# Linear attention on one core: longer load runs, one pool for PSUM tiles, a block-diagonal second matmul, and another order and another issuer at the end

The kernel runs on one core of a Trainium2 chip. The metric is the device time of one execution in microseconds (us), smaller being better.

## The reference

For each of 8 x 12 heads, with 512 rows of 64 numbers:

```python
Q_feat = np.maximum(0, Q) + 1
K_feat = np.maximum(0, K) + 1
KV = np.einsum('bhkd,bhkv->bhdv', K_feat, V)
K_sum = np.sum(K_feat, axis=2)
numerator = np.einsum('bhqd,bhdv->bhqv', Q_feat, KV)
denominator = np.einsum('bhqd,bhd->bhq', Q_feat, K_sum)
return (numerator / (denominator[:, :, :, None] + 1e-10)).astype(np.float32)
```

Q, K, V and the result are fp32 of 12.58 MB each, so 37.75 MB must be read and 12.58 MB written.

## The kernel before

It works in 12 groups of 4096 rows. Each group has three loads of 1.05 MB of fp32 that are cast to bf16 on the way (all but the first K), and one fp32 store of 1.05 MB. A *run* is the piece that is contiguous in memory: with `c` rows of 64 fp32 values per partition, 2 KB for `C = 8` and 4 KB for `C2 = 16`.

```python
C = 8; C2 = 2 * C; NP = 4; NG = 12; D1 = D + 1; W = 2 * D + 1
def view(t, c):
    return t.flatten_outer_dims().rearrange("(n p c) d -> p n c d", p=P, c=c)
q_dram = view(Q, C2); k_dram = view(K, C); v_dram = view(V, C); o_dram = view(out, C)
# ... pools; PSUM: qt 2 x 1 bank, kva 1 x 2 banks, out 2 x 2 banks

def load(g):       # K, V, Q of one group; k_raw of group 0 on nc.sync, all else on nc.gpsimd
    nc.gpsimd.dma_start(out=k_raw, in_=k_dram[:, g * NP : g * NP + NP])
    nc.gpsimd.dma_start(out=v_raw, in_=v_dram[:, g * NP : g * NP + NP])
    nc.gpsimd.dma_start(out=q_raw, in_=q_dram[:, g * 2 : g * 2 + 2])
def store(g):
    nc.gpsimd.dma_start(out=o_dram[:, g * NP : g * NP + NP], in_=outs.pop(g))

def features(g):          # VectorE: max(x + 1, 1) of K and Q; ScalarE: V into v_aug
    ...                   # beside columns of ones
def kv_and_transpose(g):  # 32 matmuls 64x128x129 into kva_ps, copied to kva (ScalarE);
    ...                   # 16 transposes of qf, copied to qt (ScalarE)
def output(g):            # h of 2: 32 matmuls of 64x64x65 into two PSUM tiles, then
    ...                   # for each tile reciprocal and multiply on VectorE into o_sb

for it in range(NG + 2):
    if it < NG: features(it)
    if 1 <= it < NG + 1: kv_and_transpose(it - 1)
    if it >= 2: output(it - 2)
    if it + IN_BUFS < NG: load(it + IN_BUFS)      # IN_BUFS = 4
    if it - LAG >= 0: store(it - LAG)             # LAG = 3
# ... the last store
```

`features`, `kv_and_transpose` and `output` each hand work to several engines. In the traces each engine's instructions stand in the order in which they are emitted: VectorE's part of output(9), for example, comes right behind the last Q feature, at 108.08 us. PSUM is the memory that holds the results of matmuls until they are copied out.

## Time and profile before

| | before |
|---|---|
| time, median of the first 3 runs | 131.68 us (130.78 to 132.09) |
| span of the profiled execution | 129.8 us |
| read + written | 37.75 + 12.58 MB, 388 GB/s over the span |
| busiest engine | ScalarE, 48% |
| DMA engines | 9 tenths or more from slice 2 to 37 of 40 |

In lines of the profile PE is TensorE (PEld its weight loads), DVE is VectorE, ACT is ScalarE, POOL is GpSimd and SP is SyncE; L93 is line 93 of that kernel, and `a<-b` says that a is written and b read. The prediction shows the busy shares, the slices and the end. Two more lines are of use. They are from the view of waits (engine and line, what was waited for: us in total, times, longest):

```profile
DVE qf L93 <- DMA q_raw<-in_Q_dram: 42.2, 12, 5.4
...
POOL out_dram L90 <- DVE o_sb L165: 19.6, 3, 10.2
```

The first is VectorE waiting for Q in each of the 12 groups: a fast engine behind a slow supply, which costs nothing as such. The second is the opposite: GpSimd could not issue three stores because the results were not there. It happens only at the end, and there the supply of work to the DMA engines is what is late.

These lines are the DMA view (packets in total; then by queue and kind, with packets, MB, and share of the 16 engines' span):

```profile
DMA packets 19213, 32.17 MB, mean 248 GB/s; under 512 B 768, under 2 KB 12544, under 8 KB 19200
...
q8 instruction: 10, 0.16, 0.5%
```

The 12,544 packets under 2 KB are mostly those of the K and V loads: 1 KB written for a run of 2 KB read. The line of queue 8 is for later: ten transfers of 16 KB that bring instructions.

### The profile page before, as it was taken

The page shows a single profiled execution, that of the slowest core. Times are in us where ns is not written, and L with a number is a line of the kernel's source. Part 1 is how long each engine was busy: PE and PEld are TensorE (multiplying, and loading weights), DVE is VectorE, ACT ScalarE, POOL GpSimd, SP SyncE. Part 2 cuts the span into 40 slices and gives each one's busy share as a digit, 9 for nine tenths or more (in the row PEclk, how much of TensorE's full clock was granted, in tenths as well). Part 3 has the DMA queues.
Part 4 walks back from the last instruction along what each step waited for, and adds up shares of the span by engine and source line. Part 5 has one row for each costly group of instructions (what it writes and reads, how often), then busy time and mean ns, then how long its engine had stood idle before and what let it go on. Part 6 is the DMA issues. An engine that isn't in the chain of part 4 may idle for free.

```text
span 129.8 us, 3048 instructions
## 1 busy us (share of the span) xinstructions
PE 59.0 (46%) x1344; PEld 50.5 (39%) x1344; DVE 57.7 (44%) x132; ACT 62.6 (48%) x73; POOL 36.1 (28%) x55
## 2 busy tenths in 40 slices
PE   0008309208758292864939119409606802933200
PEld 0007209107647191753828009308505701922100
DVE  0222212057374775727577077066227407567700
ACT  3023086590966939296690590391095096270000
POOL 6972224222332242224224222422231200202020
PEclk9999965555686959555595865875785685595555
DMA  2999999999999999999999999999999999999853
GB/s 93 321 204 195 210 194 204 210 206 211 205 209 208 209 207 206 210 207 207 277 302 207 253 331 205 231 350 191 218 347 223 212 357 418 420 417 360 341 218 121
DMA packets 19213, 32.17 MB, mean 248 GB/s; under 512 B 768, under 2 KB 12544, under 8 KB 19200
## 3 DMA queue, kind: packets, MB, share of 16 engines
q0 software_dynamic: 18672, 30.94, 106.3%
q1 hardware_dynamic: 528, 1.05, 2.1%
q8 instruction: 10, 0.16, 0.5%
q14 instruction: 3, 0.02, 0.0%
HBM read 37.75 MB, written 12.58 MB: 388 GB/s over the span
## 4 chain that ended last, share of the span: by engine, by line
DMA 72%; issue 19%; POOL 4%; POOLq 1%
DMA out_dram<-o_sb 31%; DMA k_raw<-in_K_dram 16%; DMA q_raw<-in_Q_dram 15%; DMA v_raw<-in_V_dram 9%; POOL out_dram L90 2%; POOLq L219 1%; POOL q_raw L86 1%; POOL k_raw L82 0%; POOL v_raw L85 0%; POOL identity masks.py:199 0%; POOL identity masks.py:197 0%; POOL v_aug L179 0%; POOLq L90 0%; POOLq L86 0%; POOLq L208 0%
## 5 line engine op out<-in xcount | busy, mean ns | idle before, releaser
L104 ACT COPY v_aug<-v_raw 128x1024 bf16<-128x1024 bf16 x24 | 24.1, 1056 | 48.6 <-DMA v_raw<-in_V_dram 48.6
L152 PE MATMUL o_ps<-kva,qt 64*64 64x65 bf16 x768 | 17.3, 229 | 46.9 <-DVE o_sb L165 45.8
L165 DVE TENSOR_TENSOR o_sb<-o_ps,recip 128x512 f32<-128x512 f32 x48 | 33.2, 691 | 1.6
L152 PEld LDWEIGHTS <-qt 64*64 64x64 bf16 x768 | 12.7, 137 | 52.0 <-DVE o_sb L165 48.9
L139 ACT COPY qt<-qt_ps 128x1024 bf16<-128x1024 bf16 x24 | 29.5, 1298 | 0.4
L118 PE MATMUL kva_ps<-v_aug,kf 64*128 64x129 bf16 x384 | 22.3, 302 | 15.4 <-ACT v_aug L104 10.1
L93 DVE TENSOR_SCALAR qf<-q_raw 128x2048 bf16<-128x2048 bf16 x12 | 8.3, 694 | 42.2 <-DMA q_raw<-in_Q_dram 42.2
L118 PEld LDWEIGHTS <-kf 64*128 64x128 bf16 x384 | 19.1, 137 | 16.2 <-issue 15.6
L138 PE MATMUL qt_ps<-identity,qf 128*128 128x128 bf16 x192 | 21.7, 303 | 0.1
L90 POOL DMA_DIRECT2D out_dram<-o_sb x12 | 9.3, 774 | 38.2 <-DVE o_sb L165 19.6
L138 PEld LDWEIGHTS <-qf 128*128 128x128 bf16 x192 | 18.8, 142 | 2.6 <-issue 2.2
L93 DVE TENSOR_SCALAR kf<-k_raw 128x1024 bf16<-128x1024 bf16 (+1 forms) x24 | 9.8, 450 | 11.2 <-DMA k_raw<-in_K_dram 11.1
L164 DVE RECIPROCAL recip<-o_ps 128x8 f32<-128x8 f32 x48 | 9.6, 201 | 10.5 <-PE o_ps L152 10.5
L85 POOL DMA_DIRECT2D v_raw<-in_V_dram x12 | 9.1, 759 | 17.0 <-ACT kva L127 5.4
L82 POOL DMA_DIRECT2D k_raw<-in_K_dram x11 | 8.6, 786 | 16.7 <-DVE kf L93 6.6
L86 POOL DMA_DIRECT2D q_raw<-in_Q_dram x12 | 8.4, 702 | 15.9 <-DMA k_raw<-in_K_dram 9.0
L127 ACT CAST kva<-kva_ps 64x260 bf16<-64x260 f32 x24 | 8.8, 367 | 3.5 <-PE kva_ps L118 3.4
L104 ACT ACT_TABLE_LOAD x1 | 1.3, 1283 | 0.7 <-PEq L208 0.7
masks.py:199 POOL TENSOR_SCALAR_AFFINE_SELECT identity<-identity 128x128 bf16<-128x128 bf16 x1 | 0.3, 287 | 0.1
masks.py:197 POOL MEMSET identity<- 128x128 bf16 x1 | 0.2, 244 | 0.0
L179 POOL MEMSET v_aug<- 128x16 bf16 x2 | 0.2, 175 | 0.0
L208 POOL MEMSET const-float32-0.0<- 128x1 f32 x1 | 0.1, 99 | 0.2 <-issue 0.2
(3 smaller groups left out, 0.3 us busy)
## 6 DMA issues: line engine op xcount, KB each, us to landing
out_dram<-o_sb POOLq DMA_DIRECT2D x12, 1024.0 KB, 20.0
v_raw<-in_V_dram POOLq DMA_DIRECT2D x12, 512.0 KB, 19.7
q_raw<-in_Q_dram POOLq DMA_DIRECT2D x12, 512.0 KB, 19.8
k_raw<-in_K_dram POOLq DMA_DIRECT2D x11, 512.0 KB, 19.7
k_raw<-in_K_dram SPq DMA_DIRECT2D x1, 1024.0 KB, 5.0
```

What stands on the lines that cost most here:

```text
L85: nc.gpsimd.dma_start(out=v_raw, in_=v_dram[:, g * NP : g * NP + NP])
L86: nc.gpsimd.dma_start(out=q_raw, in_=q_dram[:, g * 2 : g * 2 + 2])
L90: nc.gpsimd.dma_start(out=o_dram[:, g * NP : g * NP + NP], in_=outs.pop(g))
L93: nc.vector.tensor_scalar(out=dst, in0=src, scalar1=1.0, scalar2=1.0, op0=ALU.add, op1=ALU.max)
L104: nc.scalar.copy(out=va[:, h].rearrange("p c (n x) -> p n c x", n=2)[:, :, :, 0:D], in_=v_raw[:, h:NP:2],)
L118: nc.tensor.matmul(kva_ps[:, j, h * W : h * W + W], lhsT=kf[64 * j : 64 * j + 64, h, c, :, :], rhs=va[64 * j : 64 * j + 64, h, c, 0:W], st ...
L127: nc.scalar.copy(out=kva[64 * n : 64 * n + 64, :, :, 0:D1], in_=kva_ps[64 * n : 64 * n + 64, :, 0 : 2 * W].rearrange("p j (h x) -> p j h x ...
L138: nc.tensor.transpose(qt_ps[:, c, :], qf[:, half * C + c, :, :], identity)
L139: nc.scalar.copy(out=qt[:, :, :, half], in_=qt_ps)
L152: nc.tensor.matmul(ops[n][64 * j : 64 * j + 64, c // 4, off : off + D1], lhsT=qt[64 * n : 64 * n + 64, c, 32 * b : 32 * b + 32, :], rhs=kv ...
L164: nc.vector.reciprocal(out=recip, in_=den)
L165: nc.vector.tensor_tensor(out=o_sb[:, 2 * n + h].rearrange("p (b r) d -> p b r d", b=2), in0=num, in1=recip.to_broadcast([P, 2, 4, D]), op ...
```

## The change

Its intent: K and V in runs of 4 KB as Q has them; one block-diagonal matmul of 128 rows in place of two of 64 for each pair of heads; PSUM tiles from one pool of three; and an order of their own for the last two groups, so that VectorE's work on the third last outputs does not stand behind the last loads. The last store goes in two halves on SyncE. With these come seven output buffers for six, the features of Q in two halves, and four copies of the first matmuls' result for two. The diff is shortened (`...`).

```diff
-OUT_BUFS = 6
+OUT_BUFS = 7
-    k_dram = view(K, C)
-    v_dram = view(V, C)
+    k_dram = view(K, C2)
+    v_dram = view(V, C2)
+    psum = ... tile_pool(name="psum", bufs=3, PSUM)      # for kva_ps and o_ps; psum_kva, psum_out go
+    kva_diag = [const.tile([P, 4, 2, D1], BF16, ...) for i in range(NV)]   # zeroed once
     def store(g):
+        if g < NG - 1:
+            nc.gpsimd.dma_start(out=o_to, in_=o_sb)
+            return
+        for h in range(2):
+            nc.sync.dma_start(out=o_to[:, h:NP:2], in_=o_sb[:, h:NP:2])
     def kv_and_transpose(g):
-        # h, c of 8, j of 2: 64-row matmuls
+        # c of 16, b of 4: 32-row matmuls, one head each
+                ps = slice(32 * b, 32 * b + 32)
+                nc.tensor.matmul(kva_ps[b // 2][:, b % 2, 0:W], lhsT=kf[ps, c, :, :], rhs=va[ps, c, :], ...)
     def output(g):
-        lhsT=qt[64 * n : 64 * n + 64, c, 32 * b : 32 * b + 32, :], rhs=kva[64 * n : 64 * n + 64, j, h, 0:D1]
+        lhsT=qt[:, c, 32 * b : 32 * b + 32, :], rhs=kva[:, b]
# ...
-        for it in range(NG + 2): ...
+        for g in range(NG - 1):
+            # features(g), kv_and_transpose(g - 1), output(g - 2), load, store as before
+        kv_and_transpose(NG - 2)
+        output(NG - 3)
+        features(NG - 1)
+        output(NG - 2)
+        kv_and_transpose(NG - 1)
+        output(NG - 1)
+        for g in range(NG - 1 - LAG, NG):
+            store(g)
```

More of the change, by code (lines that the diff above doesn't have):

```diff
@@ L13 @@
 BANK = 512
-VP = 130
 IN_BUFS = 4
-OUT_BUFS = 6
+OUT_BUFS = 7
 LAG = 3
@@ L44 @@
     D1 = D + 1
-    W = 2 * D + 1
+    W = 2 * D1
     def view(t, c):
@@ L61 @@
     recip_pool = ctx.enter_context(tc.tile_pool(name="recip", bufs=4))
+    psum = ctx.enter_context(tc.tile_pool(name="psum", bufs=3, space=bass.MemoryType.PSUM))
     psum_qt = ctx.enter_context(tc.tile_pool(name="psum_qt", bufs=2, space=bass.MemoryType.PSUM))
-    psum_kva = ctx.enter_context(tc.tile_pool(name="psum_kva", bufs=1, space=bass.MemoryType.PSUM))
-    psum_out = ctx.enter_context(tc.tile_pool(name="psum_out", bufs=2, space=bass.MemoryType.PSUM))
     identity = const.tile([P, P], BF16, name="identity")
     NV = 2
-    v_aug = [const.tile([P, 2, C, VP], BF16, name=f"v_aug{i}") for i in range(NV)]
+    v_aug = [const.tile([P, C2, W], BF16, name=f"v_aug{i}") for i in range(NV)]
+    kva_diag = [const.tile([P, 4, 2, D1], BF16, name=f"kva_diag{i}") for i in range(NV)]
     raw = {}
     feat = {}
-    mid = {}
+    qts = {}
     outs = {}
@@ L77, in load @@
         k_raw = (head_pool if first else in_pool).tile(
-            [P, NP, C, D], FP32 if first else BF16, name="k_raw"
+            [P, 2, C2, D], FP32 if first else BF16, name="k_raw"
         )
-        v_raw = in_pool.tile([P, NP, C, D], BF16, name="v_raw")
+        v_raw = in_pool.tile([P, 2, C2, D], BF16, name="v_raw")
         q_raw = in_pool.tile([P, 2, C2, D], BF16, name="q_raw")
         (nc.sync if first else nc.gpsimd).dma_start(
-            out=k_raw, in_=k_dram[:, g * NP : g * NP + NP]
+            out=k_raw, in_=k_dram[:, g * 2 : g * 2 + 2]
         )
-        nc.gpsimd.dma_start(out=v_raw, in_=v_dram[:, g * NP : g * NP + NP])
+        nc.gpsimd.dma_start(out=v_raw, in_=v_dram[:, g * 2 : g * 2 + 2])
         nc.gpsimd.dma_start(out=q_raw, in_=q_dram[:, g * 2 : g * 2 + 2])
@@ L89, in store @@
     def store(g):
-        nc.gpsimd.dma_start(out=o_dram[:, g * NP : g * NP + NP], in_=outs.pop(g))
+        o_sb = outs.pop(g)
+        o_to = o_dram[:, g * NP : g * NP + NP]
+        if g < NG - 1:
[3 more added lines that the diff above has]
+            nc.sync.dma_start(out=o_to[:, h:NP:2], in_=o_sb[:, h:NP:2])
     def feature(dst, src):
@@ L98, in features @@
         k_raw, v_raw, q_raw = raw.pop(g)
-        kf = feat_pool.tile([P, 2, C, 2, D], BF16, name="kf")
+        kf = feat_pool.tile([P, C2, 2, D], BF16, name="kf")
         qf = feat_pool.tile([P, C2, 2, D], BF16, name="qf")
         va = v_aug[g % NV]
-        for h in range(2):
-            feature(kf[:, h].rearrange("p c n d -> p n c d"), k_raw[:, h:NP:2])
+        for half in range(2):
+            cs = slice(half * C, half * C + C)
+            feature(kf[:, cs].rearrange("p c n d -> p n c d"), k_raw[:, :, cs])
             nc.scalar.copy(
-                out=va[:, h].rearrange("p c (n x) -> p n c x", n=2)[:, :, :, 0:D],
-                in_=v_raw[:, h:NP:2],
-            )
-        feature(qf.rearrange("p c n d -> p n c d"), q_raw)
+                out=va[:, cs].rearrange("p c (n x) -> p n c x", n=2)[:, :, :, 0:D],
+                in_=v_raw[:, :, cs],
+            )
+        for half in range(2):
+            cs = slice(half * C, half * C + C)
+            feature(qf[:, cs].rearrange("p c n d -> p n c d"), q_raw[:, :, cs])
         feat[g] = (kf, qf)
@@ L113, in kv_and_transpose @@
         va = v_aug[g % NV]
-        kva_ps = psum_kva.tile([P, 2, BANK], FP32, name="kva_ps")
-        for h in range(2):
-            for c in range(C):
-                for j in range(2):
-                    nc.tensor.matmul(
-                        kva_ps[:, j, h * W : h * W + W],
-                        lhsT=kf[64 * j : 64 * j + 64, h, c, :, :],
-                        rhs=va[64 * j : 64 * j + 64, h, c, 0:W],
-                        start=(c == 0),
-                        stop=(c == C - 1),
-                    )
-        kva = mid_pool.tile([P, 2, 2, D1 + 1], BF16, name="kva")
-        for n in range(2):
-            nc.scalar.copy(
-                out=kva[64 * n : 64 * n + 64, :, :, 0:D1],
-                in_=kva_ps[64 * n : 64 * n + 64, :, 0 : 2 * W].rearrange(
-                    "p j (h x) -> p j h x", h=2
-                )[:, :, :, D * n : D * n + D1],
-            )
+        kva_ps = [psum.tile([P, 2, BANK], FP32, tag="ps", name="kva_ps") for _ in range(2)]
+        for c in range(C2):
+            for b in range(4):
+                ps = slice(32 * b, 32 * b + 32)
+                nc.tensor.matmul(
+                    kva_ps[b // 2][:, b % 2, 0:W],
+                    lhsT=kf[ps, c, :, :],
+                    rhs=va[ps, c, :],
+                    start=(c == 0),
+                    stop=(c == C2 - 1),
+                )
+        kva = kva_diag[g % NV]
+        for n in range(2):
+            ps = slice(64 * n, 64 * n + 64)
+            for h in range(2):
+                nc.scalar.copy(
+                    out=kva[ps, 2 * h : 2 * h + 2, n, :],
+                    in_=kva_ps[h][ps, :, D1 * n : D1 * n + D1],
+                )
         qt = mid_pool.tile([P, C, P, 2], BF16, name="qt")
@@ L139, in kv_and_transpose @@
             nc.scalar.copy(out=qt[:, :, :, half], in_=qt_ps)
-        mid[g] = (kva, qt)
+        qts[g] = qt
     def output(g):
-        kva, qt = mid.pop(g)
+        kva = kva_diag[g % NV]
+        qt = qts.pop(g)
         o_sb = out_pool.tile([P, NP, C, D], FP32, name="o_sb")
         for h in range(2):
-            ops = [psum_out.tile([P, 2, BANK], FP32, tag="o_ps", name="o_ps") for _ in range(2)]
+            ops = [psum.tile([P, 2, BANK], FP32, tag="ps", name="o_ps") for _ in range(2)]
@@ L147, in output @@
             for c in range(C):
-                off = (c % 4) * D1
-                for n in range(2):
-                    for j in range(2):
-                        b = 2 * h + j
-                        nc.tensor.matmul(
-                            ops[n][64 * j : 64 * j + 64, c // 4, off : off + D1],
-                            lhsT=qt[64 * n : 64 * n + 64, c, 32 * b : 32 * b + 32, :],
-                            rhs=kva[64 * n : 64 * n + 64, j, h, 0:D1],
-                            start=True,
-                            stop=True,
-                        )
@@ L159, in output @@
-            for n in range(2):
-                cells = ops[n][:, :, 0 : 4 * D1].rearrange("p b (r x) -> p b r x", x=D1)
-                den = cells[:, :, :, 0:1] if n else cells[:, :, :, D:D1]
-                num = cells[:, :, :, 1:D1] if n else cells[:, :, :, 0:D]
-                recip = recip_pool.tile([P, 2, 4, 1], FP32, name="recip")
-                nc.vector.reciprocal(out=recip, in_=den)
-                nc.vector.tensor_tensor(
-                    out=o_sb[:, 2 * n + h].rearrange("p (b r) d -> p b r d", b=2),
-                    in0=num,
-                    in1=recip.to_broadcast([P, 2, 4, D]),
+                for j in range(2):
+                    b = 2 * h + j
+                    nc.tensor.matmul(
+                        ops[c // 4][64 * j : 64 * j + 64, c // 2 % 2, (c % 2) * W : (c % 2) * W + W],
+                        lhsT=qt[:, c, 32 * b : 32 * b + 32, :],
+                        rhs=kva[:, b],
+                        start=True,
+                        stop=True,
+                    )
@@ new lines, in output @@
+            for i in range(2):
+                cells = ops[i][:, :, 0 : 2 * W].rearrange("p b (c n x) -> p b c n x", n=2, x=D1)
+                recip = recip_pool.tile([P, 2, 2, 2, 1], FP32, name="recip")
+                nc.vector.reciprocal(out=recip, in_=cells[:, :, :, :, D:D1])
+                nc.vector.tensor_tensor(
+                    out=o_sb[:, h:NP:2, 4 * i : 4 * i + 4].rearrange(
+                        "p n (b c) d -> p b c n d", b=2
+                    ),
+                    in0=cells[:, :, :, :, 0:D],
+                    in1=recip.to_broadcast([P, 2, 2, 2, D]),
@@ L177 @@
                 make_identity(nc, identity)
+                for t in kva_diag:
+                    nc.gpsimd.memset(t, 0.0)
                 for t in v_aug:
-                    nc.gpsimd.memset(t[:, :, :, D : D + 1], 1.0)
-        for it in range(NG + 2):
-            if it < NG:
-                features(it)
-            if 1 <= it < NG + 1:
-                kv_and_transpose(it - 1)
-            if it >= 2:
-                output(it - 2)
-            if it + IN_BUFS < NG:
-                load(it + IN_BUFS)
-            s = it - LAG
-            if s >= 0:
-                store(s)
-        for s in range(NG + 2 - LAG, NG):
-            store(s)
+                    nc.gpsimd.memset(t[:, :, D::D1], 1.0)
+        for g in range(NG - 1):
+            features(g)
+            if g >= 1:
+                kv_and_transpose(g - 1)
+            if g >= 2:
+                output(g - 2)
+            if g + IN_BUFS < NG:
+                load(g + IN_BUFS)
+            if g >= LAG:
+                store(g - LAG)
+        kv_and_transpose(NG - 2)
[6 more added lines that the diff above has]
+            store(g)
 _INS = ['Q', 'K', 'V']
```

## The prediction

> **What bounds the kernel now.** I read four views of the profile: busy shares, the span in slices, stretches of the span with their DMA rate, and the order of time at the end. First the page's busy line and two of its slice rows:
>
> ```profile
> PE 59.0 (46%) x1344; PEld 50.5 (39%) x1344; DVE 57.7 (44%) x132; ACT 62.6 (48%) x73; POOL 36.1 (28%) x55
> ...
> DMA  2999999999999999999999999999999999999853
> GB/s 93 321 204 195 210 194 204 210 206 211 205 209 208 209 207 206 210 207 207 277 302 207 253 331 205 231 350 191 218 347 223 212 357 418 420 417 360 341 218 121
> ```
>
> No engine is half busy, but the 16 DMA engines are at 9 tenths from the second slice to the last three. The rate is counted in the bytes written on chip. A load reads fp32 and writes bf16, so 206 GB/s in a load slice is 412 GB/s read from memory, and a store slice at 418 is the same traffic. The kernel is bound by 37.75 MB read plus 12.58 MB written. The stretches (columns: start:end, length, busy time of each engine with its instruction count, PE clock, DMA share, GB/s) show where that rate is lost:
>
> ```profile
> 6.50:62.50 56.00, 29.78 (x636) 25.90 (x638) 25.97 (x60) 32.62 (x38) 17.24 (x24) 0.69 1.20 206
> 62.50:98.50 36.00, 17.68 (x396) 14.92 (x390) 17.40 (x41) 19.87 (x24) 10.44 (x14) 0.69 1.15 265
> 106.50:118.50 12.00, 5.61 (x162) 4.66 (x166) 7.41 (x17) 5.76 (x7) 0.75 (x1) 0.64 1.03 418
> 118.50:122.50 4.00, 1.36 (x62) 0.94 (x54) 2.71 (x7) 0.00 (x0) 0.75 (x1) 0.50 0.92 361
> 122.50:124.50 2.00, 0.00 (x0) 0.00 (x0) 0.69 (x1) 0.00 (x0) 0.75 (x1) 0.50 0.20 80
> 124.50:127.80 3.30, 0.00 (x0) 0.00 (x0) 0.00 (x0) 0.00 (x0) 0.00 (x0) 0.50 0.84 318
> 127.80:129.80 2.00, 0.00 (x0) 0.00 (x0) 0.00 (x0) 0.00 (x0) 0.00 (x0) 0.50 0.00 0
> ```
>
> To 118.5 us the queue never runs dry. After that it does. Missing bytes against 418 GB/s: 4.0 x 57 + 2.0 x 338 + 3.3 x 100 = 1234 KB, which at 418 GB/s is **2.95 us lost**. The last packet ends near 127.7 us, and 2.05 us more pass to the span's end. The timeline of the last stores says who starves the queue (columns: start, duration, instruction, in brackets the idle time before it and what ended it):
>
> ```profile
> 101.31 0.76 DVE L93 TENSOR_SCALAR kf<-k_raw 128x1024 bf16<-128x1024 bf16 x2
> ...
> 107.47 0.69 DVE L93 TENSOR_SCALAR qf<-q_raw 128x2048 bf16<-128x2048 bf16 x1 [5.40 <-DMA q_raw<-in_Q_dram]
> 108.08 0.20 DVE L164 RECIPROCAL recip<-o_ps 128x8 f32<-128x8 f32 x1
> ...
> 112.62 0.75 POOL L90 DMA_DIRECT2D out_dram<-o_sb  x1 [10.25 <-DVE o_sb L165]
> 118.53 0.75 POOL L90 DMA_DIRECT2D out_dram<-o_sb  x1 [5.16 <-DVE o_sb L165]
> 123.49 0.75 POOL L90 DMA_DIRECT2D out_dram<-o_sb  x1 [4.21 <-DVE o_sb L165]
> ```
>
> VectorE stands idle 5.40 us for the last Q, with output(9), the third to last, queued behind that feature instruction although its inputs are there. So outputs 9, 10 and 11 all run after the last load: 108.1 to 112.4, 114.2 to 118.2 and 118.9 to 123.2. A 1 MB store drains in 1.05 MB / 418 GB/s = 2.5 us, while one output takes 4 to 5 us to compute. The queue holds several stores at 106.5 us and eats that backlog until the outputs can't keep up.
>
> **What the Trainium skill says.** (1) "DMA: Bandwidth & Descriptors", section "Bandwidth": the port ceiling is 435 GB/s, and a 16 MB load by one core reached 425. The trace agrees (411 to 418), so the rate has perhaps 2 to 4% left in it. (2) Same page, "Why small descriptors are slow (HBM only)": some 3 cycles per packet beside one per 32 bytes. Taking a run as one packet, an estimate from it: 4 KB as two runs of 2 KB costs 2 x (64 + 3) = 134 cycles, as one 128 + 3 = 131, so 2.2% less. (3) Same page, "Latency and other measured facts": first byte about 0.6 us on the hardware path and about 1 us from GpSimd. In the trace the one SyncE load starts at 0.74 us and its first packet at 1.83; the last GpSimd store starts at 123.49 and its packets near 124.4. So no gain is counted for that. (4) "TensorEngine Tiling (Array Packing)", "Key Properties": row tiles work independently. Before, 32 matmuls on two 64-row tiles take 1.92 us, 60 ns each; no trace yet shows four 32-row tiles.
>
> **The change part by part.**
> *Runs.* K and V go from four 2 KB runs per partition to two of 4 KB; Q is there already. I fitted the packet records of 17 to 98 us of the trace's own clock (6.6 to 87.6 of the span), as counts of each size per stretch of 0.5 to 3 us: 5.01 ns for a packet of 1024 bytes written (2 KB read), 9.85 (9.78 to 9.93) for a Q packet (4 KB read), 9.95 for a 4 KB store packet. Two 2 KB runs cost 10.02, one 4 KB run 9.85: 1.7%, near the page's 2.2%. K and V by GpSimd are 23 transfers of 256 such runs: 23 x 256 x 0.17 = **1.0 us saved**, all on the bounding resource. (The packets' own durations, 98 and 173 ns, would promise 12%; they overlap, shares above 1.00, so they are not what counts.)
> *Last groups' order.* Output(9) now stands ahead of features(11) on VectorE. It fits into 101 to 105 us, where VectorE stood idle for Q. Outputs 10 and 11 alone remain after the last load: output(10) from about 107.3 (Q lands about 1 us earlier), four pieces of 0.20 + 0.69 us, overlapped to about 0.85 each, done near 111. Then the last KV matmuls (1.9 us once two PSUM buffers are free near 110; they share three now), copies on ScalarE (four of 64x130; the 64x260 took 0.37 us each, so about 1.0), the two transposed-Q copies (2.45 us in all), and output(11) from 115.5 to 119.5. Allowing 1.5 us for matmuls that don't overlap, 121. The bytes left at 106.5 us, 7.28 stores x 2.51 = 18.3 us, last to 124.8 before the runs' gain, so store 10 (ready at 111) and store 11 (at 119.5 to 121) come while there is still a backlog. That gives back the **2.95 us**, less some 0.35 (my choice, from the 361 GB/s when one store is alone in flight) for the very end.
> *Last store in two halves on SyncE.* The first half can go about 1.8 us before the second. It is insurance for the order, not an added gain, since both draw on the same DMA engines.
> *Block-diagonal second matmul.* 64 matmuls of 64x64x65 a group become 32 of 128x64x130, while the first goes from 32 to 64. PE instructions stay at 1344 and the PE is 46% busy: about 0. *More kva copies, split Q features:* ScalarE +0.25 us a group (4 x 0.25 for 2 x 0.37), VectorE +0.15 us (2 x 0.42 for 0.69): 5.5 and 4.9 us of a group period of 7.6 (loads alone, 3.15 MB / 414) to 10.1 (with a store): hidden. *Two memsets of 128x520* delay the second K issue by about 1.3 us (0.24 us for 128x128), under three transfers already queued: hidden. *Seven output buffers* let output(10) and output(11) wait for stores 3 and 4 and not for 4 and 5; stores 3 and 4 land near 103 and 108 us: no wait.
> Sum: 127.7 - 2.95 + 0.35 - 1.0 = 124.1 for the last packet, + 2.05 = 126.15 span, + 1.73 (131.53 timed against 129.8 span) = 127.9; I say 128.0.
>
> **Rivals.** *A: the end stays bound by compute.* If the three shared PSUM buffers or four 32-row tiles make output(11) end at 122 to 123, about 2 us of the starvation stay: 129.5 to 130, within 2%. For it: PE, ScalarE and VectorE pass the last group in series. Against it: 2.5 to 4 us of slack against the backlog. *B: run length gives nothing, or much more.* If 4 KB runs gain 0, the time is 129.0, the edge of 2%; if the rate rose 4%, 124. The Q packets, already at 4 KB and no faster than 1.7%, speak against the second. *C: the shared PSUM stalls the steady state,* loads are issued late and the queue dries mid-span: up to 132 or 133. Against it: landing takes 20 us from issue, so eight 2.5 us transfers stand queued, and every engine is about half idle.
>
> **Range and chances.** 128.0 us against 131.68 is 2.8% faster, and faster by 2% is below 129.05. The runs of before spread by 1%. A has one chance in five, B's zero and C some one in twenty each. Range 126.5 to 129.9; faster 0.76, same 0.23, slower 0.01.
>
> **What would show it.** Right: the DMA row at 9 until the last one or two slices, no store slice below 400 GB/s between the last load and about 122 us, output(9) on VectorE before the last Q feature, load stretches at 208 to 210 GB/s and not 206, the last packet near 124. Wrong: a gap of the DMA before the last halves, VectorE waiting on PE in output(11), or a load stretch still at 206.

## The result, and the profile after

| | before | changed |
|---|---|---|
| median | 131.88 us (4 runs, 130.78 to 132.11) | 128.24 us (4 runs, 127.70 to 128.40) |
| span of the profiled execution | 129.8 us | 126.5 us |
| last data packet | 127.72 us | 125.20 us |
| last packet to end of span | 2.04 us | 1.34 us |

The ratio is 0.9732, with a 95% interval of 0.9669 to 0.9796. A ratio here is the mean time of one kernel's fast runs over that of the other's fast runs of the same rounds, so it is not quite the ratio of the medians. The forecast was 128.0 us. The time is right, but its parts are not, as the following shows.

The busy line and slices of the changed kernel:

```profile
PE 67.4 (53%) x1344; PEld 54.8 (43%) x1344; DVE 57.3 (45%) x144; ACT 64.1 (51%) x97; POOL 35.2 (28%) x56
...
DMA  3999999999999999999999999999999999999990
GB/s 75 340 211 208 212 211 213 208 212 210 214 208 211 212 209 214 209 215 208 251 336 212 229 358 209 212 365 214 210 338 249 215 306 418 420 422 405 409 356 33
```

The DMA row now holds 9 from the second slice to the last but one. A load slice moves 208 to 215 GB/s and not 194 to 211. The stretches (start:end, length, engines, clock, DMA share, GB/s), to set beside those of before:

```profile
6.50:62.50 56.00, 33.91 (x728) 28.04 (x729) 26.86 (x69) 34.39 (x52) 17.95 (x26) 0.91 1.12 212
62.50:98.50 36.00, 21.50 (x401) 17.29 (x404) 18.21 (x46) 19.80 (x31) 9.66 (x14) 0.54 1.10 267
...
106.50:118.50 12.00, 6.09 (x120) 4.83 (x120) 6.63 (x18) 3.31 (x6) 0.75 (x1) 0.64 1.02 415
118.50:122.50 4.00, 0.00 (x0) 0.00 (x0) 0.34 (x1) 0.00 (x0) 0.00 (x0) 0.50 1.02 398
122.50:124.50 2.00, 0.00 (x0) 0.00 (x0) 0.00 (x0) 0.00 (x0) 0.00 (x0) 0.50 0.40 153
124.50:126.50 2.00, 0.00 (x0) 0.00 (x0) 0.00 (x0) 0.00 (x0) 0.00 (x0) 0.50 0.03 13
```

The rate is 2.9% higher in the pure load stretch (212 for 206). Between 118.5 and 122.5 us it is 398 and not 361: no starvation. But then comes something that the prediction had not seen: from 122.5 us on the DMA engines are at work for 0.40 of the time, then 0.03, although the last data land only at 125.2 us. All instructions are done, and all stores are issued by 119.2 us, as the order of time shows:

```profile
104.65 0.69 DVE L170 TENSOR_TENSOR o_sb<-o_ps,recip 128x512 f32<-128x512 f32 x1
105.25 0.75 DVE L98 TENSOR_SCALAR kf<-k_raw 128x1024 bf16<-128x1024 bf16 x2
...
105.63 0.75 POOL L92 DMA_DIRECT2D out_dram<-o_sb  x1 [6.27 <-DVE o_sb L170]
105.92 1.02 DVE L98 TENSOR_SCALAR qf<-q_raw 128x1024 bf16<-128x1024 bf16 x2
...
110.59 0.75 POOL L92 DMA_DIRECT2D out_dram<-o_sb  x1 [4.20 <-DVE o_sb L170]
...
117.19 2.05 SPq L95 DMA_DIRECT2D out_dram<-o_sb  x2
```

Output(9) is done at 105.3 us, ahead of the last features (before: 112.3), and the last stores are issued at 105.63, 110.59, 117.19 and 118.87 us (before: 112.62, 118.53 and 123.49).

**Where the time came from.** The trace has a record of each DMA packet. I put them in order of their ends and added up the memory traffic (a cast packet counts twice its written bytes). The table gives the time at which so much had been moved, and the difference:

| MB moved | before, us | changed, us | gained so far, us |
|---|---|---|---|
| 10 | 27.26 | 26.54 | 0.72 |
| 30 | 75.76 | 74.41 | 1.35 |
| 46 | 114.59 | 112.77 | 1.82 |
| 49.5 | 125.52 | 121.31 | 4.21 |
| 50.2 | 127.36 | 123.27 | 4.09 |
| 50.33, all | 127.72 | 125.20 | 2.51 |
| end of span | 129.76 | 126.54 | 3.21 |

So the steady part gave 1.82 us (forecast 1.0). Filling the gap at the end gave another 2.4 (forecast 2.95). The very last 0.13 MB gave 1.6 back, and the end of the program returned 0.7. The forecast had 0.35 lost at the very end and nothing in the end of the program. In the last 1.4 us of transfer the packet records show about two packets in flight for most of the time, where the stretch from 106.5 to 118.5 us has 16.3 (16 engines x 1.02). The records do not name the engines; I take two packets in flight for about two engines at work.

### The profile page after: what moved, and what is told of

The parts are those of the page before. It is cut to its first block, busy times and chain, and to the rows that moved or that the text cites. A ratio compares the mean times of both kernels' runs of the same rounds, so it can differ in the third digit from the quotient of the medians.

```text
span 126.5 us, 3107 instructions
## 1 busy us (share of the span) xinstructions
PE 67.4 (53%) x1344; PEld 54.8 (43%) x1344; DVE 57.3 (45%) x144; ACT 64.1 (51%) x97; POOL 35.2 (28%) x56
## 4 chain that ended last, share of the span: by engine, by line
DMA 61%; DVE 13%; PE 8%; POOL 5%; issue 3%; ACT 2%; ACTq 1%; POOLq 0%; DVEq 0%
DMA q_raw<-in_Q_dram 46%; DMA v_raw<-in_V_dram 15%; DVE o_sb L170 9%; PE kva_ps L126 5%; PE qt_ps L146 2%; DVE recip L169 2%; DVE qf L98 2%; POOL v_raw L84 1%; POOL q_raw L85 1%; ACT qt L147 1%; POOL k_raw L81 1%; ACTq L232 1%; ACT v_aug L110 1%; PE o_ps L159 1%; POOL kva_diag L186 1%
## 5 line engine op out<-in xcount | busy, mean ns | idle before, releaser
L159 PE MATMUL o_ps<-kva_diag,qt 128*64 128x130 bf16 x384 | 22.9, 269 | 26.7 <-ACT kva_diag L137 15.9
L126 PE MATMUL kva_ps<-v_aug,kf 32*128 32x130 bf16 x768 | 24.6, 294 | 22.8 <-ACT v_aug L110 13.0
L126 PEld LDWEIGHTS <-kf 32*128 32x128 bf16 x768 | 19.7, 132 | 26.9 <-issue 14.6
L159 PEld LDWEIGHTS <-qt 128*64 128x64 bf16 x384 | 16.6, 137 | 32.7 <-issue 19.1
L98 DVE TENSOR_SCALAR qf<-q_raw 128x1024 bf16<-128x1024 bf16 x24 | 9.4, 434 | 39.0 <-DMA q_raw<-in_Q_dram 39.0
L92 POOL DMA_DIRECT2D out_dram<-o_sb x11 | 8.4, 767 | 27.9 <-DVE o_sb L170 13.6
L137 ACT CAST kva_diag<-kva_ps 64x130 bf16<-64x130 f32 x48 | 10.2, 262 | 9.1 <-PE kva_ps L126 8.8
L81 POOL DMA_DIRECT2D k_raw<-in_K_dram x11 | 7.9, 714 | 15.4 <-DMA v_raw<-in_V_dram 8.2
L186 POOL MEMSET kva_diag<- 128x520 bf16 x2 | 1.0, 528 | 0.0
```

The costliest lines, as they stand in the source:

```text
L81: (nc.sync if first else nc.gpsimd).dma_start(out=k_raw, in_=k_dram[:, g * 2 : g * 2 + 2])
L98: nc.vector.tensor_scalar(out=dst, in0=src, scalar1=1.0, scalar2=1.0, op0=ALU.add, op1=ALU.max)
L126: nc.tensor.matmul(kva_ps[b // 2][:, b % 2, 0:W], lhsT=kf[ps, c, :, :], rhs=va[ps, c, :], start=(c == 0), stop=(c == C2 - 1),)
L137: nc.scalar.copy(out=kva[ps, 2 * h : 2 * h + 2, n, :], in_=kva_ps[h][ps, :, D1 * n : D1 * n + D1],)
L159: nc.tensor.matmul(ops[c // 4][64 * j : 64 * j + 64, c // 2 % 2, (c % 2) * W : (c % 2) * W + W], lhsT=qt[:, c, 32 * b : 32 * b + 32, :], r ...
```

## The experiments

Each was timed against the kernel before in five rounds, on one chip for all runs of a call. Four calls were made (e1 to e4, e5 to e8, e9 to e11, e12); across calls only ratios are compared.

| run | median us | before in the same call | ratio (95%) |
|---|---|---|---|
| changed kernel | 128.24 | 131.88 | 0.9732 (0.9669 to 0.9796) |
| e1 order alone | 130.94 | 132.03 | 0.9924 (0.9878 to 0.9971) |
| e2 changed, old order | 128.24 | 132.03 | 0.9729 (0.9693 to 0.9764) |
| e3 changed, split, 2 KB runs | 130.83 | 132.03 | 0.9932 (0.9892 to 0.9973) |
| e4 changed, split, 4 KB runs | 129.83 | 132.03 | 0.9833 (0.9780 to 0.9885) |
| e5 changed, last store on GpSimd | 129.62 | 131.49 | 0.9870 (0.9831 to 0.9910) |
| e6 changed, 64x64 second matmul | 128.21 | 131.49 | 0.9755 (0.9720 to 0.9791) |
| e7 the same, old order | 128.29 | 131.49 | 0.9761 (0.9721 to 0.9800) |
| e8 order and SyncE halves alone | 129.78 | 131.49 | 0.9871 (0.9829 to 0.9913) |
| e9 last two stores on SyncE | 127.69 | 131.62 | 0.9708 (0.9657 to 0.9758) |
| e10 the same, last half cut at 112 | 128.33 | 131.62 | 0.9759 (0.9710 to 0.9808) |
| e11 half of first matmuls (wrong result) | 126.86 | 131.62 | 0.9658 (0.9607 to 0.9710) |
| e12 the same, groups 0 to 5 only (wrong result) | 127.93 | 131.81 | 0.9765 (0.9703 to 0.9828) |

The medians of before take in all 11 executions of a call. Of these 1, 1, 2 and 5 are slow ones in the four calls, which the ratios leave out.

### e1 and e2: the order of the last groups, alone and undone

e1 is the kernel before with the new loop and seven output buffers. e2 is the changed kernel with the old loop:

```diff
+        for it in range(NG + 2):
+            if it < NG: features(it)
+            if 1 <= it < NG + 1: kv_and_transpose(it - 1)
+            if it >= 2: output(it - 2)
+            # ... load and store as before
-        for g in range(NG - 1): ...
-        kv_and_transpose(NG - 2); output(NG - 3); features(NG - 1)
-        output(NG - 2); kv_and_transpose(NG - 1); output(NG - 1)
```

> The kernel before with the new order of the last two groups and seven output buffers alone (2 KB runs, 64x64 matmuls, whole last store on GpSimd). Theory P (the prediction): the starvation of 2.95 us goes and 0.35 comes back at the very end, so about 2.6 us less, 129.1 against 131.7. Theory S (skew: the DMA engines have drifted apart by up to 2 us by the end, and the last store then ends on the slowest of them): the gap moves from before the last store to after it, so about 1.3 to 1.6 us less, 130.2.

> The changed kernel with the old order of the last groups, all else kept. P: the runs' 1.0 us alone stay, about 130.7 (2.6 us slower than the changed kernel). S: the runs give 1.8 us as the moved bytes show, and the SyncE end some 0.6 us, so about 129.3, some 1.2 us slower than the changed kernel.

e1 gained 1.0 us, less than either theory said. The gap closed there only in part (49.5 MB at 123.89 us, 1.62 before the kernel before), and the slowest engines then ended at 127.14 us, only 0.58 earlier. The last output is ready at 121.4 us, later than the forecast 119.5 to 121, its store is issued at 121.68, and the rate drops ahead of it:

```profile
118.50:122.50 4.00, 0.65 (x30) 0.51 (x30) 2.11 (x5) 0.00 (x0) 0.75 (x1) 0.50 0.91 370
122.50:124.50 2.00, 0.00 (x0) 0.00 (x0) 0.00 (x0) 0.00 (x0) 0.00 (x0) 0.50 0.81 317
```

In shorter stretches it is 328 GB/s from 121 to 122 us and 156 from 122 to 123. By the prediction's own count that is (90 + 262) KB / 418 GB/s, or some 0.8 us of starvation left.

e2 refuted both: no loss shows (0.9729 against 0.9732). A pair agrees: e6 and e7, below, differ in the order alone, and have 128.21 and 128.29 us. e2's stores are indeed issued late, as the GpSimd part of its timeline shows:

```profile
98.60 0.75 POOL L92 DMA_DIRECT2D out_dram<-o_sb  x1 [3.15 <-DVE o_sb L170]
109.61 0.75 POOL L92 DMA_DIRECT2D out_dram<-o_sb  x1 [10.25 <-DVE o_sb L170]
116.02 0.75 POOL L92 DMA_DIRECT2D out_dram<-o_sb  x1 [5.66 <-DVE recip L169]
```

Store 9 at 109.61 us instead of 105.63, store 10 at 116.02 instead of 110.59. The idle time of 10.25 us is the same as the kernel before's at that place. Yet the last result is ready at 119.1 us (118.8 with the new order), since VectorE does the eight pieces of outputs 10 and 11 back to back at 0.84 us each, from 112.3 to 119.1 us. Before, two pieces at a time were followed by a wait for the tensor engine of 0.5 to 0.7 us, and the same two outputs took from 114.2 to 123.2 us. First two such starts of before, then two pieces of e2:

```profile
116.47 0.21 DVE L164 RECIPROCAL recip<-o_ps 128x8 f32<-128x8 f32 x1 [0.53 <-PE o_ps L152]
...
118.94 0.21 DVE L164 RECIPROCAL recip<-o_ps 128x8 f32<-128x8 f32 x1 [0.71 <-PE o_ps L152]
```

```profile
113.97 0.20 DVE L169 RECIPROCAL recip<-o_ps 128x8 f32<-128x8 f32 x1
114.20 0.69 DVE L170 TENSOR_TENSOR o_sb<-o_ps,recip 128x512 f32<-128x512 f32 x1
114.81 0.20 DVE L169 RECIPROCAL recip<-o_ps 128x8 f32<-128x8 f32 x1
115.04 0.69 DVE L170 TENSOR_TENSOR o_sb<-o_ps,recip 128x512 f32<-128x512 f32 x1
```

So in the changed kernel the order is worth nothing that these runs can show: another part does its work too (49.5 MB at 121.44 us in e2, 121.31 in the changed kernel).

### e3 and e4: the length of the runs

The changed kernel with each K and V load cut into two DMAs, by halves of the rows (2 KB runs) or by blocks (4 KB runs), the arithmetic being the same:

```diff
-        nc.gpsimd.dma_start(out=v_raw, in_=v_dram[:, g * 2 : g * 2 + 2])
+        for h in range(2):   # e3; K likewise
+            nc.gpsimd.dma_start(out=v_raw[:, :, h * C : h * C + C], in_=v_dram[:, g * 2 : g * 2 + 2, h * C : h * C + C])
+        for h in range(2):   # e4
+            nc.gpsimd.dma_start(out=v_raw[:, h : h + 1], in_=v_dram[:, g * 2 + h : g * 2 + h + 1])
```

> The changed kernel with each K and V load cut into two DMAs by halves of the rows of a partition, so that its runs are 2 KB again; to be compared with the next one, which has as many DMAs with 4 KB runs. P: 1.0 us slower than the next. Accounting of the moved bytes: 1.8 us slower. If run length does nothing: the same.

> The changed kernel with each K and V load cut into two DMAs by block, runs still 4 KB: the control of the one before it. Both theories: within 0.5 us of the changed kernel (128.2), unless the shorter queue of eight half-size transfers lets the DMA engines run dry.

The timed difference is 1.0 us, what the prediction said, but by a coincidence. The pure load stretch of e3, then of e4:

```profile
6.50:62.50 56.00, 31.75 (x678) 26.18 (x682) 26.44 (x68) 34.42 (x51) 28.06 (x39) 0.80 1.20 206
```

```profile
6.50:62.50 56.00, 34.32 (x712) 28.50 (x713) 26.91 (x69) 35.54 (x52) 23.45 (x40) 0.72 1.12 210
```

With 2 KB runs the rate is that of the kernel before, 206; with 4 KB it is 210. At 46 MB e4 is 1.84 us ahead of e3. At the end of the two profiled executions only 0.27 us of it is left (spans of 128.61 and 128.88 us); e5 shows what takes part of it. e4's profiled execution is the slowest of its six, which lie between 128.49 and 130.38 us, a wider spread than in the other runs, so the medians say more about the end. e4 missed its own expectation too: it is 1.6 us slower than the changed kernel (two calls), part of it in that same end.

A cleaner size of the runs in place comes from e8 and e6, which share a call. They have the same order, the same SyncE halves and the same 64x64 second matmul. They differ in the runs and in what these bring along (32-row first matmuls, shared PSUM pool, split Q features): 129.78 against 128.21 us, 1.6 us less, and e6 is 1.57 us ahead at 46 MB already. So the gain lies in the steady state.

### e5 and e8: the last store

e5 is the changed kernel with one line for all stores, on GpSimd. e8 is e1 with the SyncE halves added.

```diff
-        if g < NG - 1:
-            nc.gpsimd.dma_start(out=o_to, in_=o_sb)
-            return
-        for h in range(2):
-            nc.sync.dma_start(out=o_to[:, h:NP:2], in_=o_sb[:, h:NP:2])
+        nc.gpsimd.dma_start(out=o_to, in_=o_sb)
```

> The changed kernel with its last store whole and on GpSimd again. If the SyncE halves are only an insurance, as the prediction says: within 0.3 us of 128.2. If the end of the program waits for GpSimd to drain its own last transfer (before: 1.54 us from the last landing to the span's end, changed: 0.95 us): 0.6 us slower, 128.8.

> The kernel before with the new order, seven buffers and the two SyncE halves (2 KB runs, 64x64 matmuls). Beside the order alone (130.9): insurance theory 130.9; end-of-program theory 0.6 us less, and the first half's earlier start up to 0.7 us less again: 129.6 to 130.3.

e5 is 129.62 us, a ratio of 0.9870 where the changed kernel has 0.9732. e6, which was timed in the same call and has the halves, has 128.21 us, 1.41 less. The "insurance" is worth about 1.4 us, though e5's last packet ends at 124.56 us, 0.64 *earlier* than in the changed kernel. What comes after it shows in the view of the program's last line, in the row of GpSimd's DRAIN (shortest/median/longest in ns, first and last start in us). In order: before, changed, e5, e3, e4.

```profile
L219 POOLq DRAIN  x3: 51/95/5529, 123.5 to 129.5; - x3
```

```profile
L232 POOLq DRAIN  x3: 51/102/15211, 110.6 to 126.3; - x3
```

```profile
L228 POOLq DRAIN  x3: 51/87/8050, 118.9 to 127.4; - x3
```

```profile
L232 POOLq DRAIN  x3: 51/88/14462, 112.8 to 128.6; - x3
```

```profile
L232 POOLq DRAIN  x3: 51/88/16240, 111.6 to 128.3; - x3
```

A DRAIN is the instruction on which GpSimd stands here from about its last issue on (110.57 us in the changed kernel, whose last GpSimd store is issued at 110.59). The longest of the three is this wait at the program's end, and the first start is its own: 118.9 us plus 8.05 gives 126.94 us in e5. Beside the last landing of a GpSimd transfer, which the trace has too:

| | last GpSimd landing | drain ends | between | last landing of all |
|---|---|---|---|---|
| before | 128.22 | 129.00 | 0.78 | 128.22 |
| e1, 2 KB runs | 127.58 | 128.36 | 0.78 | 127.58 |
| e8, 2 KB runs | 125.00 | 125.74 | 0.74 | 127.13 |
| e3, 2 KB runs, split | 126.43 | 127.29 | 0.86 | 128.00 |
| changed, 4 KB runs | 123.85 | 125.78 | 1.92 | 125.59 |
| e5, 4 KB runs | 124.97 | 126.94 | 1.97 | 124.97 |
| e4, 4 KB runs, split | 124.99 | 127.86 | 2.86 | 126.73 |

GpSimd's drain ends 0.74 to 0.86 us after its last landing in the kernels with 2 KB runs, and 1.9 to 2.9 us after it in those with 4 KB runs. So the longer runs carry a cost of their own at the end. With the last 1 MB on SyncE the drain runs beside it and ends at 125.78 us, next to SyncE's own last landing of 125.59: all but 0.2 us of it is hidden. e8 beside e1 has the halves where the drain is short: ratios of 0.9871 and 0.9924 (two calls), a difference of 0.0053, or 0.7 us. The two intervals overlap, so this value is not established. In the traces the time from the last landing to the end of the span falls from 1.54 to 0.89 us. But the halves do a second thing there: the first is issued at 119.41 us and fills the gap that e1 has left (415 GB/s from 118.5 to 122.5 us, where e1 has 370). That the runs change the drain is measured, e3 and e4 having equally many DMAs; *why* they do is not known. It also fits e4: its drain ends at 127.86 us, 1.13 us after the last landing of all, and so takes back part of what its runs gained.

### e6 and e7: the block-diagonal matmul

The second matmul as 64 of 64x64x65 again, with the shared PSUM pool kept; in e7 with the old order too.

```diff
-                    lhsT=qt[:, c, 32 * b : 32 * b + 32, :], rhs=kva[:, b],
+                for n in range(2):
# ... for j in range(2), b = 2 * h + j, a matmul with
+                        ops[n][64 * j : 64 * j + 64, c // 4, off : off + D1],
+                        lhsT=qt[64 * n : 64 * n + 64, c, 32 * b : 32 * b + 32, :],
+                        rhs=kva[64 * n : 64 * n + 64, b, :],
# ... kva is a tile of [P, 4, D1]; VectorE's pieces go by n as before
```

> The changed kernel with the second matmul as 64 of 64x64x65 a group again, two PSUM tiles filled together, the new order kept. The prediction (this part worth about 0): 128.2. If the new matmul's earlier first tile is what lets VectorE run pieces back to back at 0.84 us: output(11) ends near 121 and not 118.8, still inside the backlog, so at most 0.6 us slower, 128.2 to 128.8.

> The one before it with the old order of the last groups as well. If either the new order or the overlapped outputs is enough to keep the queue full (so that the old order alone cost nothing), taking both away brings the gap back: 1 to 1.5 us slower than the changed kernel, 129.2 to 129.7. If the order is worth nothing at all: 128.2 to 128.8, as the one before it. The prediction's sum (order alone 2.6 us): 130.8.

e6 is 128.21 us: no gain of this part shows, as predicted. e7 was to bring the gap back and didn't: 128.29 us, last output at 119.6 us. Its VectorE pieces, too, follow each other at 0.84 us. So it isn't the block-diagonal form that overlaps the outputs. What e7 still has and the kernel before hasn't is the shared pool of three two-bank PSUM tiles (before: two for the outputs), 4 KB runs with loads that land earlier (the last Q is there at 105.1 us, before at 107.5), the 32-row first matmuls, the features of Q in halves, the seventh output buffer and the SyncE halves. Other traces narrow this. e1 and e8, which have the seventh buffer and e8 the SyncE halves, keep the waits of 0.5 to 0.7 us; e3, with 2 KB runs, has none (its last four pieces start 0.84 us apart). So neither the buffer nor the halves nor the runs removed them. That the third PSUM buffer did is likely from e7's timeline, in which most of the next half's matmuls run after the first of two pieces (before: after the second), but no run isolates it from the 32-row matmuls and the halved features.

### e9 and e10: two attempts at the tail

e9 sends the last two stores by SyncE. e10 also cuts the last half at partition 112, which spreads its bytes over the DMA engines in another way.

```diff
         if g < NG - 1:
-            nc.gpsimd.dma_start(out=o_to, in_=o_sb)
+            (nc.gpsimd if g < NG - 2 else nc.sync).dma_start(out=o_to, in_=o_sb)
             return
```

> The changed kernel with the last two stores, not the last alone, on SyncE, so that GpSimd's last transfer lands near 121 us and its final drain (1.92 us after that landing in the changed kernel) is over well before the last data land. If the drain and the interleaving of two queues cost something at the end: up to 0.6 us less, 127.6. If the end is set by the slowest DMA engines alone: the same, 128.2.

> The one before it, with the last half store cut into partitions 0 to 111 and 112 to 127, so that the bytes of the last half fall on the DMA engines in another way. If the engines that finish last (some two of 16, for 1.6 us) are those that the second cut relieves: about 1 us less than the one before. If they are others: the same or 0.2 us more.

e9 is the fastest correct kernel, 127.69 us. GpSimd's drain now ends at 124.65 us, 0.6 us before the last landing of 125.23. Its ratio lies 0.0024, some 0.3 us, below the changed kernel's. They were timed in different calls and the intervals overlap, so its lead is not established. e10 is slower than e9 by 0.6 us (one call): cutting the last half there didn't relieve the engines that are late.

### e11 and e12: which engines are late, and why

Both leave out half of the first matmuls (the result is wrong), e11 in all groups and e12 in groups 0 to 5. In e11 1344 pairs of weight load and matmul become 960 (the figures "1536 to 1152" in its expectation are a slip).

```diff
-        for c in range(C2):
+        for c in range(C2 // 2):                        # e11
+        for c in range(C2 // 2 if g < NG // 2 else C2):  # e12
```

> Wrong on purpose: the changed kernel with half of the first matmuls left out, so that the tensor engine's instructions fall by 1536 to 1152 matmul and weight-load pairs fewer, and with them the 16 KB instruction transfers (10 in the changed kernel, each some 0.95 us of one DMA engine's time) to about 6 or fewer. If those transfers are what makes some engines late at the end: the trickle of two engines shrinks from 1.6 to below 1 us and the time falls by 0.4 to 1 us. If it is the engines themselves: the trickle and the time stay within 0.2 us.

> Wrong on purpose: the changed kernel with half of the first matmuls left out in the first six groups only. The instruction transfers fall from 10 to 8 or 9, the work of the last six groups is as in the changed kernel. If the number of those transfers is what makes engines late: the stretch from the last time that 12 engines are at work to the last packet lies between 0.95 us (7 transfers) and 2.25 us (10), about 1.5, and the time near 127.5. If only what happens late counts: 2.1 to 2.3 us, and 128.0 to 128.3.

In e11 the instruction transfers fall from 10 to 7, and the time to 126.86 us. From the last moment with 12 packets in flight to the last packet, which I call the trickle, it takes 0.95 us (changed kernel 2.25). Its last stretches:

```profile
118.50:122.50 4.00, 0.00 (x0) 0.00 (x0) 0.00 (x0) 0.00 (x0) 0.00 (x0) 0.50 1.02 399
122.50:124.50 2.00, 0.00 (x0) 0.00 (x0) 0.00 (x0) 0.00 (x0) 0.00 (x0) 0.50 0.23 87
124.50:126.50 2.00, 0.00 (x0) 0.00 (x0) 0.00 (x0) 0.00 (x0) 0.00 (x0) 0.50 0.00 0
```

At 50.2 MB e11 is only 0.56 us ahead of the changed kernel, at the last packet 1.59: the trickle is what went. This looked like proof that instruction transfers make some engines late. But e12 has 9 transfers and keeps a trickle of 2.05 us and a time of 127.93 us, and e6 and e7, which have 13, show 2.35 and 2.10 us, no more than the changed kernel with 10. The number of transfers alone therefore doesn't order the runs. A dip ahead of the last store matters as well: counted in the same way, the trickle is about 0.1 us in the kernel before, with its gap, 1.4 in e1, with what is left of it, and 1.3 in e5, with a dip to 324 GB/s from 120 to 121 us. The runs without a dip show 2.0 us or more, e11 apart. That fits engines which have drifted apart and start level again after a gap; it is also why e5's last packet can end earlier than the changed kernel's. In e11 the last instruction transfer starts at 106.5 us, in all the others between 113 and 118 us. A late transfer of 1.0 us on one engine with nothing behind it to even it out would fit, and so would the lighter tensor engine in the last six groups. Which of these it is stays open.

## Why the prediction was right, and where its parts were not

- *What bounds the kernel.* Right: the DMA row stays at 9, no engine exceeds 53%, and every gain or loss is found in the moved bytes or after the last of them.
- *Runs: 1.0 us.* The direction was right, and so was the place, the steady load stretch; the size was too small. The step that failed is the fit: 9.85 ns for a 4 KB load packet, taken from Q packets among shorter ones. The Q packets of the kernel before do not fix it well: fitted again, in stretches of 0.5 to 3 us, they give 9.84 to 10.02 ns. The same fit over the changed kernel gives 9.78 ns, for Q as well (9.77 to 9.79). So 23 x 256 runs save 10.02 - 9.78 = 0.24 ns each, 1.4 us, and the 3072 Q packets 0.2 us; measured were 1.82 us in the changed kernel and 1.6 between e8 and e6.
- *Order of the last groups: 2.95 us.* The gap did close, and 2.4 us came back by 49.5 MB. But the order, named as the cause, is not needed for it: undone alone it costs nothing that shows (e2, 0.9729). Nor is it enough: done alone it leaves some 0.8 us of the starvation and gives 1.0 us of time (e1). The step "done near 111 ... from 115.5 to 119.5" described the output times well (118.8), and overlapped pieces of 0.85 us were in it (0.84 measured). But the order does not bring this overlap: in e1 the pieces still wait, and output(11) ends at 121.4 us. And with such pieces the old order is fast enough too: 119.1 us (e2). So the 2.95 us were credited to the wrong part.
- *The very end: 0.35 us.* Sized wrong: 1.6 us. I read the 361 GB/s from 118.5 to 122.5 us as the rate of one store alone. In shorter stretches it is 401 to 406 from 120 to 122 us, with dips before and after (326 and 274), in which some engines have run out of work and others have not: from 122.3 to 124.5 us the packets in flight fall from 16 to 1. So in the kernel before this loss lies inside the gap ahead of the last store, which the engines then begin nearly together (from 0 to 16 packets in flight between 124.8 and 125.0 us). Close the gap and it comes out at the very end: the trickle grows from 0.1 us in the kernel before to 2.25 in the changed one.
- *SyncE halves: no gain.* This step is wrong. They take GpSimd's drain off the end and are worth about 1.4 us with 4 KB runs, whose drain is longer, and with 2 KB runs 0.7 us, not clear of noise, part of it by filling the gap of e1. "+ 2.05" after the last packet became 1.34. The reading "its packets near 124.4" is wrong as well: those are the last of the store before, and the last store's own start at 124.81 us, 1.3 after its issue (SyncE's load: 1.1). Nothing was counted on it.
- *Block diagonal, kva copies, memsets, split features: hidden.* Right (e6: 128.21 us for the matmul). The 64 first matmuls on four 32-row tiles take 1.9 us a group, as the 32 on two tiles did; that the tiles work side by side, as the Trainium skill has it ("TensorEngine Tiling (Array Packing)", "Key Properties"), agrees with that.
- *Rivals.* A did not occur in the changed kernel: the queue stayed full. With the order alone (e1) it did occur in part, with output(11) ending at 121.4 us. C did not occur: the steady stretches got faster. Of B, the load rate rose by 2.9% in the pure load stretch, between the 1.7% of the sum and the 4% of the rival.

That the sum was right is luck, since errors cancel: runs +0.8 and end of program +0.7 us better than forecast, gap 0.55 and very end 1.3 worse: some 0.35 us off in all, near the 0.39 of the spans (126.54 against the forecast 126.15).

## What to carry to other kernels

When DMA is the bound, add up the moved bytes over time for both kernels: it shows in one table which stretch a change helped, and what it gave back. Undo each part alone in the *changed* kernel before crediting it, since two parts can do the same work: here the new order (e8) and the overlapped outputs (e2) each kept the queue full, beside the SyncE halves. And look past the last byte: which engine issued the last transfer and whether it went whole or in halves changed the time by about 1.4 us here.

## What the Trainium skill lacked or had wrong

- "DMA: Bandwidth & Descriptors", "Issuing engines are not separate DMA queues": it says that issuing on another engine only saves the sequencer's time. Here the last store in halves on SyncE and not on GpSimd saved about 1.4 us (128.24 against 129.62 in e5, two calls; e6, in e5's call, 128.21), and in e5 GpSimd's drain lasts 1.97 us past the last landing.
- No page found says how long GpSimd's drain at a program's end lasts past its last transfer, or that this depends on the loads: 0.74 to 0.86 us after GpSimd's last landing with 2 KB runs of cast loads, 1.9 to 2.9 us with 4 KB runs.
- "DMA: Bandwidth & Descriptors", "Why small descriptors are slow (HBM only)": the estimate drawn from it, 2.2% for 4 KB runs against 2 KB, is near the fitted 2.4% (10.02 ns for two packets of 2 KB runs against 9.78 for one of 4 KB). What it doesn't say is that this is still worth some 1.6 us of 130 at runs as long as these (e8 against e6).
- Same page, "Latency and other measured facts": it has two of 16 DMA engines usually slower. The traces would agree in number (about two packets in flight over most of the last 1.4 us), but tell neither which engines nor why; with fewer matmuls the tail shrank from 2.25 to 0.95 us (e11), which the page doesn't lead one to expect.
